# Output projection of a hybrid decoder layer from seven products of half-size blocks

## The chip, the cores and the metric

The kernel runs on one core of a Trainium2 chip. A core has TensorE (matrix products into eight PSUM banks of 128 x 512 floats), VectorE and ScalarE (elementwise work, both reach PSUM), GpSimd (elementwise work in SBUF) and SyncE, whose queue (SP) issues the DMA transfers here. Each engine works through its own queue in order; semaphores order the queues among each other. The metric is the device time of one execution in microseconds.

## The reference

One layer on x of 512 x 1024 floats: RMSNorm, one input projection, four mLSTM heads and eight attention heads, and an output projection with the residual:

```
h = rmsnorm(x, norm_w);  proj = h @ w_in            # 1024 x 4616
y_ml = rmsnorm(sigmoid(o) * mlstm(q, k, v, i, f)) * silu(z)     # 512 x 512, 4 heads of 128
y_at = moba_attention(q, k, v) * silu(z)                        # 512 x 512, 8 heads of 64
out  = x + concat([y_ml, y_at], -1) @ w_out         # (512 x 1024) @ (1024 x 1024)
```

The last line is what the change rewrites.

## The kernel before

All large products are made from float32 split in two parts: hi is the value rounded to fp32r, lo is the rest. `mm3` (L343) adds three products into a bank: hi x hi, hi x lo, lo x hi. A right side of 512 columns is the widest one.

Weights come in pieces of 128 x 1024 (two k-tiles of 512 columns). `load_w` (L221) issues a piece's DMA into one of three `raw` tiles; `g_split` (L237) makes `whi` on ScalarE (a cast) and `wlo` on VectorE (raw minus hi), with six tiles of each. The main stream emits the projections in the order z, aq, ak, av, qk0, qk1, mo, mv, az; everything beside it (evacuation, attention, mLSTM heads, weight splits) is written as Python generators that the class `Plan` resumes when an estimate of time says that what they wait for is there. So the order in each engine's queue comes from that planner.

The end of the program: the four mLSTM heads (`g_mlstm`) are normalised on VectorE, with a small power on GpSimd (tile `mst`), transposed on TensorE, and `put_y` makes hi and lo of the left side in `br` tiles. `ev_z` does the same for the attention half in `cv`, then `xh` and `xl`. The output projection (`out_mm`, L848) runs over two halves of 512 columns, four row blocks of 128 and eight k-tiles: 4 x 8 x 3 = 96 products of 512 columns for each half, and the last row block of the second half in two pieces of 256 columns, so that its last add and store are short. `ev_out` adds the residual, loaded to `tq` and `tk`, and issues the store:

```
    for ks in ((0, 1, 2, 3), (4, 5, 6, 7)):
        for t in range(NT):
            for k in ks:
                out_mm(ps4[t], 0, t, k)
```

Of the kernel before, what the change touches and what calls it, by code (L numbers as in the profile page):

```python
# [10 lines left out]
F32 = mybir.dt.float32  # L11
F32R = mybir.dt.float32r
# [4 lines left out]
P = 128  # L17
D = 1024
S = 512
# [32 lines left out]
class Engine:  # L52
    """Issues to one engine and keeps an estimate of when it gets through."""

# [74 lines left out]


@with_exitstack
def hybrid_layer(ctx: ExitStack, tc: tile.TileContext, xT, x, w_in, w_out, smalls, out):
# [48 lines left out]

    # the table of Silu and the clock of TensorE come up while the first loads run
    rstdb = sb("rstdb", [P, S])
# [9 lines left out]

    # ---- weights, in pieces of two k-tiles
    pieces = []
    off = 0
    for name, cols in _chunks():
        n = len(cols)
        for kk in range(4):
            pieces.append((name, kk, n, w_in, off))  # L200
# [9 lines left out]
    W = {}  # L210
    raws = {}
    nload, nsplit = [0], [0]

    def src_ap(i):
        _, _, n, src, o = pieces[i]
        return bass.AP(tensor=src.tensor, offset=src.offset + o, ap=[[2 * n, P], [1, 2 * n]])

    def pair(t, n):
        return t[:, :2 * n].rearrange("p (k n) -> p k n", k=2)

    def load_w(dst=None, between=None):  # L221
        i = nload[0]
        if i >= len(pieces) or (dst is None and i - max(nsplit[0], 5) >= 3):
# [11 lines left out]
        raws[i] = pair(dst, n)  # L235

    def g_split(i, copy=act.copy, parts=1):  # L237
        name, kk, n, _, _ = pieces[i]
        raw = raws.pop(i)
# [7 lines left out]
        load_w()  # L247

    def split_w():
        i = nsplit[0]  # L250
        if i < len(pieces):
            nsplit[0] += 1
            plan.add(g_split(i), rank=1)
# [17 lines left out]

    # ---- long-lived tiles
    sz = sb("sz", [P, NT, 512])
# [79 lines left out]
    def feat_mm(ps, name, f, k):  # L353
        hi, lo = need_w(name, k // 2)
        fs = slice(f * P, (f + 1) * P)
        mm3(ps, hi[:, k % 2, fs], lo[:, k % 2, fs], xh[:, k], xl[:, k], k == 0, k == KT - 1)

    def main_bank():
        plan.until(banks.ok)
        return banks.get()  # L360

    def group(g, mul, evac):
# [61 lines left out]

    # ---- gates of the mLSTM heads
    def g_rstdb():
# [66 lines left out]

    # ---- attention
    pts = {}
# [146 lines left out]

    # ---- mLSTM
    yh, yl = {}, {}

    def put_y(f, src, scale, t_=0.0):
        hi, lo = (br.get(), br.get()) if f < 4 else (xh[:, f - 4], xl[:, f - 4])
        if scale is None:
            yield act.copy(hi, src)
            t_ = dve.tensor_tensor(lo, src, hi.bitcast(F32), op=ALU.subtract)  # L650
        else:
            yield act.activation(hi, src, AF.Copy, scale=scale)
            t_ = dve.scalar_tensor_tensor(lo, src, scale, hi.bitcast(F32), op0=ALU.mult, op1=ALU.subtract)
        yh[f], yl[f] = hi, lo
        yield t_

    def g_mlstm(h):
# [99 lines left out]
        yield plan.now + SLACK  # L757
        for t_ in put_y(h, ps, sm[:, C_MN + h:C_MN + h + 1]):
            yield t_
# [4 lines left out]
    def ev_z(f):  # L764
        z = cv[f // 2][:, f % 2]

        def ev(ps):
            t_ = dve.tensor_tensor(z, ps, rstdb, op=ALU.mult)
            banks.put(t_, ps)
            yield t_  # L770
            yield act.activation(z, z, AF.Silu)
            t_ = dve.tensor_tensor(z, z, ot[:, f], op=ALU.mult)
            yield when(lambda: have["proj"], t_)
            for t_ in put_y(4 + f, z, None):
                yield t_
        return ev

    have["proj"] = 0

    # ---- main stream  # L780
    psz = [[banks.get() for _ in range(2)] for _ in range(NT)]
# [60 lines left out]
    tok_chunk("mv", lambda t: ev_scale(mv[:, t, :, 0:128], t, "mv", MLH))  # L842
    plan.until(lambda: have["silu"] == 3)
    for f in range(4):
        group(f, lambda ps, k: feat_mm(ps, "az", f, k), ev_z(f))
    have["proj"] = 1

    def out_mm(ps, half, t, k, c0=0, c1=512):  # L848
        plan.until(lambda: k in yh)
        hi, lo = need_w(f"wo{half}", k // 2)  # L850
        ts = slice(t * P, (t + 1) * P)
        mm3(ps[:, :c1 - c0], yh[k][:, ts], yl[k][:, ts], hi[:, k % 2, c0:c1], lo[:, k % 2, c0:c1],
            k == 0, k == KT - 1)

    xres = []
    plan.until(lambda: have["y"] == MLH)
    for half in range(2):
        r = tk if half else tq
        for t in range(NT):
            nc.sync.dma_start(r[:, t], x[t * P:(t + 1) * P, half * 512:half * 512 + 512])  # L860
        xres.append([r[:, t] for t in range(NT)])

    def ev_out(half, t, c0=0, c1=512):
        def ev(ps):
            o = xres[half][t][:, c0:c1]
            t_ = dve.tensor_tensor(o, ps[:, :c1 - c0], o, op=ALU.add)
            banks.put(t_, ps)
            nc.sync.dma_start(out[t * P:(t + 1) * P, half * 512 + c0:half * 512 + c1], o)
            yield t_
        return ev  # L870

    ps4 = [main_bank() for _ in range(NT)]
    for ks in ((0, 1, 2, 3), (4, 5, 6, 7)):
        for t in range(NT):
            for k in ks:
                out_mm(ps4[t], 0, t, k)
                plan.run()
        for _ in range(2):
            split_w()
    for t in range(NT):  # L880
        plan.add(ev_out(0, t)(ps4[t]), rank=0, ready=plan.now + SLACK)
    for t in range(NT):
        cols = ((0, 512),) if t < NT - 1 else ((0, 256), (256, 512))
        for c0, c1 in cols:
            ps = main_bank()
            for k in range(KT):
                out_mm(ps, 1, t, k, c0, c1)
                plan.run()
            plan.add(ev_out(1, t, c0, c1)(ps), rank=0, ready=plan.now + SLACK)
    plan.until(lambda: not plan.programs)  # L890

# [35 lines left out]
```

## Time and profile before

| what | us |
|---|---|
| median of 3 runs (310.26 to 310.55) | 310.38 |
| span of the profiled execution | 308.8 |
| TensorE busy | 303.2 |
| VectorE busy | 185.8 |
| ScalarE busy | 150.2 |
| GpSimd busy | 58.3 |

The span is that of one profiled execution, from its first instruction to its last; the runs are timed without a profile. Busy time of TensorE counts pipelined products, so it says that TensorE never waits, not that it is at its peak. All helpers of VectorE, ScalarE and GpSimd record line 75; they are told apart by their tiles.

### The profile page before, as it was taken

The page shows a single profiled execution, that of the slowest core. Times are in us where ns is not written, and L with a number is a line of the kernel's source. Part 1 is how long each engine was busy: PE and PEld are TensorE (multiplying, and loading weights), DVE is VectorE, ACT ScalarE, POOL GpSimd, SP SyncE. Part 2 cuts the span into 40 slices and gives each one's busy share as a digit, 9 for nine tenths or more (in the row PEclk, how much of TensorE's full clock was granted, in tenths as well). Part 3 has the DMA queues.
Part 4 walks back from the last instruction along what each step waited for, and adds up shares of the span by engine and source line. Part 5 has one row for each costly group of instructions (what it writes and reads, how often), then busy time and mean ns, then how long its engine had stood idle before and what let it go on. Part 6 is the DMA issues. An engine that isn't in the chain of part 4 may idle for free.

```text
span 308.8 us, 4284 instructions
## 1 busy us (share of the span) xinstructions
PE 303.2 (98%) x1594; PEld 248.2 (80%) x1594; DVE 185.8 (60%) x395; ACT 150.2 (49%) x271; POOL 58.3 (19%) x94
## 2 busy tenths in 40 slices
PE   7999999999999999999999999999999999999995
PEld 3999888778888868886886888688889978788885
DVE  4892458935456549999627995501568999714111
ACT  3372754314365671775439356899763237420000
POOL 3000164262501800450150005110000060000000
PEclk9999999999999999999999999999999999999999
DMA  7997122141410410132103021400252102832101
GB/s 198 394 412 300 68 69 75 63 137 49 155 70 0 168 39 9 60 128 78 68 2 137 0 83 55 138 0 2 93 176 73 44 24 72 306 135 102 36 34 68
DMA packets 10821, 31.80 MB, mean 103 GB/s; under 512 B 1328, under 2 KB 1584, under 8 KB 10800
## 3 DMA queue, kind: packets, MB, share of 16 engines
q1 hardware_dynamic: 10800, 31.53, 28.8%
q8 instruction: 12, 0.20, 0.3%
q14 instruction: 9, 0.07, 0.1%
HBM read 29.42 MB, written 2.10 MB: 102 GB/s over the span
## 4 chain that ended last, share of the span: by engine, by line
PE 95%; DMA 2%; SPq 1%; DVE 1%; ACT 0%; issue 0%
PE bank L173 89%; PE bank L177 6%; DMA tq<-in_xT_dram 2%; ACT xh L75 0%; DVE wlo L75 0%; SPq L306 0%; DVE xl L75 0%; SPq L234 0%; SPq L232 0%; DVE tk L75 0%; SPq L230 0%; SPq L180 0%
## 5 line engine op out<-in xcount | busy, mean ns | idle before, releaser
L173 PE MATMUL bank<-whi,xh 128*128 128x512 f32 (+2 forms) x260 | 86.4, 367 | 0.7 <-DVE whi L75 0.7
L173 PE MATMUL bank<-wlo,xh 128*128 128x512 f32 (+2 forms) x260 | 85.1, 363 | 0.2 <-DVE wlo L75 0.2
L173 PE MATMUL bank<-whi,xl 128*128 128x512 f32 (+2 forms) x260 | 85.2, 363 | 0.0
L75 DVE TENSOR_TENSOR wlo<-raw,whi 128x1024 fp32r<-128x1024 f32 x39 | 48.0, 1241 | 10.8 <-ACT whi L75 9.2
L173 PEld LDWEIGHTS bank<-whi,xh 128*128 128x128 f32 x260 | 45.1, 188 | 8.7 <-ACT xh L75 1.1
L173 PEld LDWEIGHTS bank<-whi,xl 128*128 128x128 f32 x260 | 45.0, 188 | 8.1
L173 PEld LDWEIGHTS bank<-wlo,xh 128*128 128x128 f32 x260 | 45.1, 188 | 7.9 <-DVE wlo L75 0.6
L75 ACT CAST whi<-raw 128x1024 fp32r<-128x1024 f32 x39 | 40.8, 1048 | 19.8 <-PE bank L173 11.5
L173 PE MATMUL bank<-xh,whi 128*128 128x512 f32 x96 | 40.9, 426 | 0.0
L173 PE MATMUL bank<-xh,wlo 128*128 128x512 f32 x96 | 37.9, 395 | 0.0
L173 PE MATMUL bank<-xl,whi 128*128 128x512 f32 x96 | 37.7, 393 | 0.0
L75 POOL TENSOR_SCALAR b<-b,rec 128x128 f32<-128x128 f32 (+3 forms) x32 | 18.9, 612 | 84.6 <-DVE rec L75 67.1
L75 ACT ACTIVATE br<-bank,sm 64x512 fp32r<-64x512 f32 (+1 forms) x28 | 19.1, 684 | 14.7 <-DVE br L75 9.7
L173 PEld LDWEIGHTS bank<-xh,whi 128*128 128x128 f32 x96 | 18.2, 190 | 4.5 <-issue 2.1
L173 PE MATMUL bank<-whi,br 128*128 128x512 f32 (+1 forms) x72 | 21.4, 370 | 0.0
L173 PEld LDWEIGHTS bank<-xh,wlo 128*128 128x128 f32 x96 | 18.0, 188 | 4.2
L75 ACT ACTIVATE b<-b,mn 128x128 f32<-128x128 f32 (+3 forms) x32 | 17.6, 553 | 7.6 <-DVE mn L75 7.5
L173 PEld LDWEIGHTS bank<-xl,whi 128*128 128x128 f32 x96 | 18.2, 189 | 2.5
L75 DVE SCALAR_TENSOR_TENSOR br<-bank,sm,br 64x512 fp32r<-64x512 f32 (+1 forms) x20 | 15.0, 749 | 5.9 <-ACT br L75 5.6
L75 DVE CUSTOM_DVE_ANT_0 b<-bank,b 128x128 f32<-128x128 f32 (+3 forms) x32 | 14.2, 488 | 5.5 <-PE bank L173 5.4
L173 PEld LDWEIGHTS bank<-whi,br 128*128 128x128 f32 x72 | 13.1, 188 | 2.6
L177 PEld LDWEIGHTS bank<-ident,b 128*128 128x128 f32 (+1 forms) x104 | 12.3, 140 | 3.4 <-issue 0.4
(141 smaller groups left out, 374.1 us busy)
## 6 DMA issues: line engine op xcount, KB each, us to landing
raw<-in_w_in_dram SPq DMA_DIRECT2D x31, 512.0 KB, 3.2
raw<-in_w_out_dram SPq DMA_DIRECT2D x8, 512.0 KB, 3.5
b<-in_w_in_dram SPq DMA_DIRECT2D x3, 520.0 KB, 7.5
tq<-in_xT_dram SPq DMA_DIRECT2D x4, 256.0 KB, 5.4
tk<-in_xT_dram SPq DMA_DIRECT2D x4, 256.0 KB, 7.8
ot<-in_x_dram SPq DMA_DIRECT2D x2, 512.0 KB, 9.1
cv<-in_x_dram SPq DMA_DIRECT2D x2, 512.0 KB, 9.9
tq<-in_x_dram SPq DMA_DIRECT2D x4, 256.0 KB, 5.8
```

Of the source, the lines that this page charges most:

```text
L75: fn(out, *args, **kw)
L173: nc.tensor.matmul(out_, lhsT=lhsT, rhs=rhs, start=start, stop=stop, skip_group_check=True)
L177: nc.tensor.transpose(out_, in_, idn)
```

## The change

The 512 x 1024 by 1024 x 1024 product is cut in four blocks on each side (left: rows in two halves r, k in two halves; right: k in two halves r, columns in two halves c) and made from seven products of half-size blocks, p5, p1, p2, p6, p3, p7 and p4 in that order. Each is 256 rows by 512 k by 512 columns: 2 row blocks x 4 k-tiles x 3 = 24 products of 512 columns. The right sides are weight blocks or sums of two of them; the sums are made on GpSimd, 128 x 1024 at a time, and then split in hi and lo as before. The left sides are blocks of y, or sums and differences of them: differences of the mLSTM and the attention half on VectorE (`b<-tq,cv`), three more combinations on GpSimd (L1117), and each is split in hi and lo. Each product is added to or subtracted from the residual's tiles (`res`, named `b` in the rows) on VectorE; some banks collect two products first. Output weights are loaded in blocks, some of them twice. `Stage` is a list scheduler: it takes tasks with an engine, a cost and what they come after, and emits them by start and longest tail; the whole last stage goes through it. The first two products' weights, and the p5 left side, are prepared by the planner as before.

```diff
+class Stage:
...
+        for t in order:
+            t["tail"] = t["cost"] + max([t["lat"] + u["tail"] for u in t["next"]], default=0.0)
...
+                start = max(free.get(e, 0.0), min(t["ready"] for t in can))
+                t = max((t for t in can if t["ready"] <= start), key=lambda t: (t["tail"], -t["n"]))
...
-    off = 0
-    for half in range(2):
-        for kk in range(4):
-            pieces.append((f"wo{half}", kk, 512, w_out, off))
-            off += P * 2 * 512
...
+    PRODS = [("p5", [(0, 0), (0, 1)]), ("p1", [(0, 0)]), ("p2", [(0, 0), (1, 0)]), ("p6", [(0, 0), (1, 1)]),
+             ("p3", [(0, 1), (1, 1)]), ("p7", [(1, 1)]), ("p4", [(1, 0), (1, 1)])]
...
+        if name in OVER:
+            src = B.pop((*OVER[name], u))
+            pair_ = [B.get(b, src) for b in blocks]
+            t_ = pool.tensor_tensor(src, *pair_, op=ALU.subtract if name == "p6" else ALU.add)
...
+        yield act.copy(hi, src)
+        t_ = dve.tensor_tensor(lo, src, hi.bitcast(F32), op=ALU.subtract)
...
-            t_ = dve.scalar_tensor_tensor(lo, src, scale, hi.bitcast(F32), op0=ALU.mult, op1=ALU.subtract)
...
+        yield dve.tensor_tensor(lo(h), yml[:, h, H[1]], hi(h).bitcast(F32), op=ALU.subtract)
...
+    CHAIN = {"p5": ("B", (1, 1, ADD, False)), "p1": ("A", (0, 0, ADD, False)),
+             "p2": ("1", (0, 0, ADD, True)), "p6": ("A", (0, 1, SUB, False)),
+             "p3": ("B", (0, 1, ADD, True)), "p7": ("A", (1, 1, SUB, True)),
+             "p4": ("A", (1, 0, ADD, True))}
...
+        last = PARTS[q] = st.add("PE", 3 * 231.0 * (q[4] - q[3]) / 512, part(*q), [last], lat=0.0)
...
+        BL[tag] = st.add("SP", 1450.0, dma(dst, w_src(*blk)), after, lat=2500.0)
...
+                sums[name, u] = t_ = st.add("POOL", 2250.0, lambda src=src, w2=w2, op=op: nc.gpsimd.tensor_tensor(src, src, w2, op=op), dep)
...
+            last = st.add("ACT", 1050.0, f_hi, dep)
+            lows[name, u] = t_ = st.add("DVE", 1240.0, f_lo, [last])
...
+        h_ = st.add("ACT", n, lambda: nc.scalar.copy(hi, src), [*dep, *war])
+        l_ = st.add("DVE", n + 10, lambda: nc.vector.tensor_tensor(lo, src, hi.bitcast(F32), op=SUB), [h_, *war])
...
+    t_ = st.add("DVE", 690.0, vec(z3, ps3, rstdb, ALU.mult), at=300.0)
...
+        x1.append(st.add("DVE", 420.0, vec(xav[:, f], yml[:, f, H[0]], y_at[f][:, H[0]]), z))
+        xs1.append(split("p1", f, xav[:, f], [x1[f]]))
+        split("p2", f, y_at[f][:, H[0]], z)
+        split("p4", f, y_at[f][:, H[1]], z)
...
+        r_ = st.add("POOL", 1200.0, gps(xrv[:, ks], yml[:, ks, H[1]], xav[:, ks]), x1[ks])
+        s_ = split("p6", ks, xrv[:, ks], [r_])
...
+        c_ = st.add("POOL", 1200.0, gps(xav[:, ks], yml[:, ks, H[0]], yml[:, ks, H[1]]), [r_, *xs1[ks]])
...
+        e_ = st.add("POOL", 1200.0, gps(xrv[:, ks], xrv[:, ks], cv[u][:, :, H[1]]), [s_, zdone])
...
+        t_ = st.add("DVE", 80 + 1.2 * (c1 - c0), ev_prod(bank[key, a][:, c0:c1], d, op), [*deps, RL[r, c, a], old])
```

What stands on VectorE in the output stage before: the low parts of the attention half (`xl`), weight splits (`wlo`), and adds from banks into the residual.

```order
L75 SCALAR_TENSOR_TENSOR br_83<-bank_87,sm,br_84 128x512
L75 TENSOR_TENSOR cv_132<-bank_93,rstdb 128x512
L75 TENSOR_TENSOR xl<-cv_131,xh 128x512 x2
L75 TENSOR_TENSOR xl<-cv_132,xh 128x512
L75 TENSOR_TENSOR cv_132<-cv_132,ot 128x512
L75 TENSOR_TENSOR xl<-cv_132,xh 128x512
L75 TENSOR_TENSOR wlo<-raw,whi 128x1024 x2
L75 TENSOR_TENSOR tq<-bank_91,tq 128x512
```

And now, from the last head's low part on, the first twelve of 37 rows up to the last weight split:

```order
L75 TENSOR_TENSOR br_81<-tq,br_85 128x256 x2
L1114 TENSOR_TENSOR b_3_72<-tq,cv_131 128x256 x2
L1114 TENSOR_TENSOR cv_132<-bank_91,rstdb 128x512
L1123 TENSOR_TENSOR br_84<-b_3_72,br_82 128x256 x2
L1114 TENSOR_TENSOR b_3_72<-tq,cv_132 128x256
L1123 TENSOR_TENSOR xl<-cv_131,xh 128x256
L1114 TENSOR_TENSOR cv_132<-cv_132,ot 128x512
L1123 TENSOR_TENSOR xl<-cv_131,xh 128x256
L1114 TENSOR_TENSOR b_3_72<-tq,cv_132 128x256
L1123 TENSOR_TENSOR br_83<-b_3_72,br_79 128x256
L1104 TENSOR_TENSOR wlo<-raw,whi 128x1024
L1123 TENSOR_TENSOR br_83<-b_3_72,br_79 128x256
```

Differences of left sides, more low parts at half width and ten weight splits stand on VectorE now where four splits and a few low parts stood.

GpSimd at the end of the program before; `mst` is the small power of each head, and nothing follows the fourth:

```order
L75 AFFINE_SELECT b_1_70<-b_1_70 128x512
L75 TENSOR_SCALAR mst<-mst 128x4
L75 TENSOR_TENSOR mst<-mst,mhalf 128x4
```

And now, from the last head's power on (the first product's two sums stand ahead of the powers):

```order
L75 TENSOR_TENSOR mst<-mst,mhalf 128x4
L75 TENSOR_TENSOR raw<-raw 128x1024
L1117 TENSOR_TENSOR b_4_73<-tq,b_3_72 128x512
L1117 TENSOR_TENSOR b_3_72<-tq 128x512
L1092 TENSOR_TENSOR sz<-sz,raw 128x1024
L1092 TENSOR_TENSOR raw<-raw,sz 128x1024
L1092 TENSOR_TENSOR raw<-raw,vbuf 128x1024
L1117 TENSOR_TENSOR b_4_73<-tq,b_3_72 128x512
L1092 TENSOR_TENSOR vbuf<-vbuf,sz 128x1024
L1092 TENSOR_TENSOR tk<-tk,vbuf 128x1024
```

Fourteen sums of 128 x 1024 or 128 x 512 follow the heads' powers where nothing did; the last five of them are not shown.

## Rows read from the trace of the kernel before

**Rows 1.** The page: span, and busy time of TensorE.

```profile
span 308.8 us, 4284 instructions
PE 303.2 (98%) x1594; PEld 248.2 (80%) x1594; DVE 185.8 (60%) x395; ACT 150.2 (49%) x271; POOL 58.3 (19%) x94
```

**Rows 2.** The chain that ended last, merged: start us, us, what.

```profile
258.58 46.75 PE bank L173 x225
...
305.35 0.42 DVE tk L75
```

**Rows 3.** Stretches: us; PE, PEld, DVE, ACT, POOL busy (x); PEclk; DMA share; GB/s.

```profile
260.00:270.00 10.00, 10.00 (x44) 7.98 (x43) 8.13 (x11) 4.00 (x6) 0.00 (x0) 1.00 0.85 283
...
290.00:300.00 10.00, 10.00 (x47) 8.22 (x46) 1.02 (x2) 0.00 (x0) 0.00 (x0) 1.00 0.14 52
300.00:309.00 9.00, 5.32 (x45) 5.11 (x44) 1.22 (x3) 0.00 (x0) 0.00 (x0) 0.96 0.16 58
```

**Rows 4.** Timeline of TensorE, output stage's first and last product: start us, us, what.

```profile
260.51 0.39 PE L173 MATMUL bank<-whi,br 128*128 128x512 f32 x1
...
305.04 0.28 PE L173 MATMUL bank<-whi,xl 128*128 128x256 f32 x1
```

**Rows 5.** Groups by line and shape from 225 us: busy us, mean ns.

```profile
L75 DVE TENSOR_TENSOR wlo<-raw,whi 128x1024 fp32r<-128x1024 f32 x10 | 12.0, 1219 | 0.3 <-ACT whi L75 0.3
L75 ACT CAST whi<-raw 128x1024 fp32r<-128x1024 f32 x8 | 8.3, 1046 | 5.5 <-issue 3.0 <-DMA raw<-in_w_out_dram 2.1 <-PE bank L173 0.5
L75 DVE TENSOR_TENSOR tk<-bank,tk 128x512 f32<-128x512 f32 x3 | 2.1, 692 | 12.3 <-PE bank L173 12.3
L75 DVE TENSOR_TENSOR tk<-bank,tk 128x256 f32<-128x256 f32 x2 | 0.8, 425 | 4.6 <-PE bank L173 4.6
```

**Rows 6.** Timeline of VectorE in the output stage.

```profile
261.32 0.75 DVE L75 SCALAR_TENSOR_TENSOR br<-bank,sm,br 128x512 fp32r<-128x512 f32 x1
...
262.58 1.89 DVE L75 TENSOR_TENSOR xl<-cv,xh 128x512 fp32r<-128x512 f32 x3
...
283.64 2.35 DVE L75 TENSOR_TENSOR wlo<-raw,whi 128x1024 fp32r<-128x1024 f32 x2
```

**Rows 7.** Timelines of VectorE and GpSimd where both read SBUF.

```profile
104.46 1.73 DVE L75 TENSOR_TENSOR wlo<-raw,whi 128x1024 fp32r<-128x1024 f32 x1 [1.35 <-PE bank L173]
104.48 0.63 POOL L75 TENSOR_SCALAR b<-dist 128x512 f32<-128x512 f32 x1
105.20 1.47 POOL L75 TENSOR_SCALAR b<-dist 128x512 f32<-128x512 f32 x1
118.57 2.33 DVE L75 SCALAR_TENSOR_TENSOR cv<-xp,sm,cv 128x512 f32<-128x512 f32 x3
131.84 2.99 DVE L75 SCALAR_TENSOR_TENSOR cv<-xp,sm,cv 128x512 f32<-128x512 f32 x3 [0.45 <-ACT cv L75]
132.14 1.13 POOL L75 TENSOR_SCALAR b<-b,rec 128x512 f32<-128x512 f32 x1
158.35 0.63 POOL L75 TENSOR_SCALAR b<-dist 128x512 f32<-128x512 f32 x1
```

**Rows 8.** The same two timelines where neither was stretched.

```profile
49.46 1.65 POOL L75 TENSOR_TENSOR rq<-rq,mhalf 128x8 f32<-128x8 f32 x1
49.88 1.23 DVE L75 TENSOR_TENSOR wlo<-raw,whi 128x1024 fp32r<-128x1024 f32 x1 [0.26 <-ACT whi L75]
81.41 0.63 POOL L75 TENSOR_SCALAR b<-dist 128x512 f32<-128x512 f32 x1
81.48 0.69 DVE L75 TENSOR_TENSOR tk<-bank,rq 128x512 f32<-128x512 f32 x1 [1.91 <-POOL rq L75]
```

**Rows 9.** Timeline of GpSimd, the first head's power near the end.

```profile
246.66 0.20 POOL L75 TENSOR_SCALAR mst<-mst 128x4 f32<-128x4 f32 x1 [39.66 <-DVE mst L75]
```

**Rows 10.** Timeline of TensorE, the program's first products (on zeros).

```profile
1.24 3.90 PE L191 MATMUL bank<-rstdb 128*128 128x512 bf16 x10 [1.24 <-DVE warm L187]
```

**Rows 11.** The page's DMA issues: count, KB each, us from issue to landing.

```profile
raw<-in_w_out_dram SPq DMA_DIRECT2D x8, 512.0 KB, 3.5
```

More of the change, by code (lines that the diff above doesn't have):

```diff
@@ L128, in put, with __init__, add, run @@
         self.free.extend([when, t] for t in tiles)
+class Stage:
+    def __init__(self):
+        self.tasks = []
+    def add(self, eng, cost, fn, after=(), at=0.0, lat=220.0):
+        t = {"eng": eng, "cost": cost, "fn": fn, "after": [a for a in after if a], "at": at, "lat": lat, "n": len(self.tasks)}
+        self.tasks.append(t)
+        return t
+    def run(self, clocks):
+        for t in self.tasks:
+            t["next"], t["left"], t["ready"] = [], len(t["after"]), t["at"]
+        last = None
+        for t in self.tasks:
+            for a in t["after"]:
+                a["next"].append(t)
+        order, seen = [], {}
+        def visit(t):
+            if seen.get(t["n"]):
+                return
+            seen[t["n"]] = 1
+            for u in t["next"]:
+                visit(u)
+            order.append(t)
+        for t in self.tasks:
+            visit(t)
+        for t in order:
+            t["tail"] = t["cost"] + max([t["lat"] + u["tail"] for u in t["next"]], default=0.0)
+        free, done, todo = dict(clocks), [], {t["n"]: t for t in self.tasks}
+        while todo:
+            best = None
+            for e in {t["eng"] for t in todo.values()}:
+                can = [t for t in todo.values() if t["eng"] == e and not t["left"]]
+                if not can:
+                    continue
+                start = max(free.get(e, 0.0), min(t["ready"] for t in can))
+                t = max((t for t in can if t["ready"] <= start), key=lambda t: (t["tail"], -t["n"]))
+                if best is None or start < best[0]:
+                    best = (start, t)
+            start, t = best
+            del todo[t["n"]]
+            free[t["eng"]] = start + t["cost"]
+            done.append((start, t))
+            for u in t["next"]:
+                u["left"] -= 1
+                u["ready"] = max(u["ready"], start + t["cost"] + t["lat"])
+        for start, t in done:
+            t["start"] = start
+            t["fn"]()
+        return done
 @with_exitstack
@@ L210, in hybrid_layer @@
     W = {}
+    NREG = sum(p[3] is w_in for p in pieces)
     raws = {}
@@ L252, in split_w @@
             nsplit[0] += 1
-            plan.add(g_split(i), rank=1)
+            plan.add(g_split(i) if i < NREG else g_osplit(i), rank=1)
     def need_w(name, kk):
@@ L757, in g_mlstm @@
         yield plan.now + SLACK
-        for t_ in put_y(h, ps, sm[:, C_MN + h:C_MN + h + 1]):
+        yield when(lambda: have["S"] == MLH)
+        if "p5" not in X:
+            X["p5"] = two([br.get() for _ in range(2)]), two([br.get() for _ in range(2)])
+        for t_ in put_ml(h, ps, sm[:, C_MN + h:C_MN + h + 1]):
             yield t_
@@ L857, in hybrid_layer @@
[L857 to L889, printed above, removed]
@@ L890, in hybrid_layer, with ev_keep @@
-    plan.until(lambda: not plan.programs)
+    for j in range(len(LOADS)):
+        plan.add(g_load(j), rank=1)
+    def ev_keep(ps):
+        zlast.append(ps)
+        yield 0.0
+    for f in range(NT):
+        group(f, lambda ps, k: feat_mm(ps, "az", f, k), ev_z(f) if f < 3 else ev_keep)
+    plan.until(lambda: have["y"] == MLH and have["zat"] == 3 and zlast and ("p1", 1) in W and (1, 0, 0) in B)
+    st = Stage()
+    ADD, SUB = ALU.add, ALU.subtract
+    NAMES = [n for n, _ in PRODS]
+    xa, xr = b5.get()[:, 0:1024], b5.get()[:, 0:1024]
@@ new lines, in hybrid_layer, with part, fn @@
+    bank = {}
+    for key in "BA1":
+        for a in range(2):
+            bank[key, a] = main_bank()
+    PARTS = {}
+    seq = []
+    for name in NAMES:
+        wide = [(a, k, 0, 512) for k in range(4) for a in range(2)]
+        if name in ("p7", "p4"):
+            wide = [(a, k, c0, c1) for a in range(2)
+                    for c0, c1 in (((0, 256), (256, 512)) if name == "p4" and a else ((0, 512),)) for k in range(4)]
+        seq += [(name, *w) for w in wide]
+    def part(name, a, k, c0, c1):
+        def fn():
+            key = "1" if (name, c0) == ("p4", 256) else CHAIN[name][0]
+            hi, lo = W[name, k // 2]
+            xs = X[name]
+            ts = slice(a * P, (a + 1) * P)
+            mm3(bank[key, a][:, c0:c1], xs[0](k)[:, ts], xs[1](k)[:, ts], hi[:, k % 2, c0:c1], lo[:, k % 2, c0:c1],
+                k == 0 and (name in ("p5", "p1", "p2") or key == "1"), k == 3)
+        return fn
@@ new lines, in hybrid_layer, with parts, before @@
+    last = None
+    for q in seq:
+        last = PARTS[q] = st.add("PE", 3 * 231.0 * (q[4] - q[3]) / 512, part(*q), [last], lat=0.0)
+    def parts(name, **kw):
+        names = ("name", "a", "k", "c0")
+        return [t for q, t in PARTS.items() if q[0] == name and all(q[names.index(n)] == v for n, v in kw.items())]
+    def before(task, consumers):
+        for c in consumers:
+            c["after"].append(task)
+    rooms = [t[:, 1024 * u:1024 * u + 1024] for t in (flat(sz), vbuf, flat(tk), flat(ot)) for u in range(2)]
@@ new lines, in dma, with w_src, load, load_res @@
+    def dma(out_, in_):
+        return lambda: nc.sync.dma_start(out_, in_)
+    def w_src(r, c, u):
+        return bass.AP(tensor=w_out.tensor, offset=w_out.offset + (c * 4 + 2 * r + u) * P * 1024, ap=[[1024, P], [1, 1024]])
+    BT, BL = {}, {}
+    def load(tag, blk, dst, after=()):
+        BT[tag] = dst
+        BL[tag] = st.add("SP", 1450.0, dma(dst, w_src(*blk)), after, lat=2500.0)
+    def load_res(r, c):
+        for a in range(2):
+            t_ = 2 * r + a
+            RL[r, c, a] = st.add("SP", 730.0, dma(res[r, c, a], x[t_ * P:(t_ + 1) * P, c * 512:c * 512 + 512]), lat=2500.0)
@@ new lines, in vec, with gps, split @@
+    def vec(out_, a, b, op=SUB):
+        return lambda: nc.vector.tensor_tensor(out_, a, b, op=op)
+    def gps(out_, a, b, op=SUB):
+        return lambda: nc.gpsimd.tensor_tensor(out_, a, b, op=op)
+    def split(name, ks, src, dep, war=()):
+        hi, lo = X[name][0](ks), X[name][1](ks)
+        n = 410.0 if isinstance(ks, int) else 650.0
+        h_ = st.add("ACT", n, lambda: nc.scalar.copy(hi, src), [*dep, *war])
+        l_ = st.add("DVE", n + 10, lambda: nc.vector.tensor_tensor(lo, src, hi.bitcast(F32), op=SUB), [h_, *war])
+        for k in ([ks] if isinstance(ks, int) else range(ks.start, ks.stop)):
+            before(l_, parts(name, k=k))
+        return l_
@@ new lines, in hybrid_layer @@
+    for name in NAMES:
+        key, (r, c, op, end) = CHAIN[name]
+        for a in range(2):
+            if name == "p4" and a:
+                result(name, r, c, op, a, 256, 512, key, parts("p7", a=a), False)
+                result(name, r, c, op, a, 0, 256, key, parts(name, a=a, c0=0), True)
+                result(name, r, c, op, a, 256, 512, "1", parts(name, a=a, c0=256), True)
+                continue
+            t_ = result(name, r, c, op, a, 0, 512, key, parts(name, a=a), end)
+            if name in AFTER:
+                before(t_, parts(AFTER[name], a=a))
+            if name == "p2" and a:
+                before(t_, parts("p4", a=a, c0=256))
```

172 lines of the change are left out of this document (144 added, 28 removed).

## The prediction

> **What bounds the kernel now.** I read the page first, then the chain, then a table by stretches, then single rows of the last 50 us. The page gives TensorE 303.2 of 308.8 us busy [rows 1], and the chain's last long piece is one uninterrupted run of products from 258.58 to 305.33, followed only by one add on VectorE and its store [rows 2]. The table says the same of the stage that the change rewrites: from 260 on TensorE is busy in every stretch, at a granted clock of 1.00 until it stops, while VectorE's 8 us in 10 fall to 1 and GpSimd does nothing [rows 3]. So the output stage is bound by its count of products. Its first product starts at 260.51 and its last ends at 305.32 [rows 4]: 44.8 us for 192 products of 512 columns (the last row block's 48 products have 256 columns and count half), that is 0.2334 us each. After it come 3.5 us until the span's end at 308.8 (add, store, landing), which any version pays. The page's execution has a span of 308.8 us; the median of the runs is 310.38, so 1.6 us are added to a span to get a time.
>
> **Products.** Seven half-size products of 24 each are 168, so 24 go: 24 x 0.2334 = 5.6 us less. If TensorE never waited, the stage would take 168 x 0.2334 = 39.2 us. Ahead of the stage one weight split of 1.22 us now stands between the last heads' normalisations on VectorE, and TensorE's transposes wait for these; I charge half of it, 0.6 us (0 to 1.2). With TensorE alone the change is therefore worth -5.6 + 0.6 = -5.0.
>
> **What VectorE gets.** By the order it has 42 instructions from the last head's low part to its last weight split, where before it had 20 in the whole rest of the program. Durations start to start: a split of 128x1024 takes 1.13, with the hand-overs 1.14 (two in 2.35 [rows 6] less the 1.22 of one [rows 5]), a 512 wide one 0.60 (three in 1.89 [rows 6] less the 0.69 of one); a 256 wide one lasts 0.425 where a 512 wide one lasts 0.692 [rows 5], so 0.33 start to start (estimate). The list: 10 weight splits = 11.4; 7 of 512 columns with two operands in SBUF = 4.2; 18 of 256 columns, two operands in SBUF = 5.9; 7 of 512 columns that read a PSUM bank = 4.2. Sum 25.7 us. If nothing else held it, VectorE would be through its last split at about 261.7 + 25.7 = 287.4, some 7 us before the seventh product starts (261.1 + 144 x 0.2334 = 294.7), and all of it would be hidden under the products.
>
> **What GpSimd gets, and the port.** Thirteen of the sums fall in the same stretch: 7 of 128x1024 and 6 of 128x512, all reading SBUF twice. The trace of before has no such sum. What it has is GpSimd reading SBUF beside VectorE, and there the two take turns [rows 7]. At 104.46 a weight split, 1.22 elsewhere, lasted 1.73; a GpSimd instruction of 0.63 began 0.02 later and ran at full speed; the next one, again 0.63 alone (158.35), lasted 1.47 and ended 0.48 after the split. So the split waited for the first and the second waited for the split. At 131.84 three VectorE instructions with both operands in SBUF took 2.99 instead of the 2.33 of the same three at 118.57, and the first of the GpSimd ones between them, at 132.14, 1.13 instead of 0.63. Where VectorE reads a PSUM bank and a small operand, both ran at full speed (81.41 and 81.48) [rows 8]. So I take the two engines' SBUF reads as exclusive, instruction by instruction, in order of arrival. Then 35 of VectorE's 42 instructions (21.5 us) and all 13 sums share one resource.
>
> The Trainium skill (SBUF — State Buffer, "Who interferes with whom") states this as a rule that speaks against the change: a VectorE instruction with two SBUF inputs and a GpSimd instruction that reads SBUF exclude each other for a whole instruction, and the first to come goes first. The rows at 104.46 agree. The row at 49.46 agrees only in part: a GpSimd power over 128x8 lasted 1.65 us and a weight split that began at 49.88 kept its 1.23 [rows 8], so what is held seems to be the reading, not the instruction; a sum reads to its end, so by either reading it holds.
>
> Price of a sum. Lower end: one pass over 1024 elements, twice the 0.63 of a GpSimd instruction over 512 [rows 7], 1.26 us. Upper end: two operands read one after the other, 2.52 us. A gain is no end here, since an instruction more on an engine that waits for the port gives nothing back. I take 2.25 (1.2 for 512 columns), near the upper end, because both operands have to be read and because the change's own list of costs, which charges 2250 and 1200 ns, is within 2% of the rows wherever a row exists (cast 1050 for 1.046, weight split 1240 for 1.219, add 690 for 0.692) [rows 5].
>
> The Trainium skill (GPSIMD Engine Reference, "Elementwise — side-by-side cycle accounting") gives 4497 ns for a two-input add of 2048 elements a partition; an estimate from that page is 2.25 us for 1024, which would give the same sum as below.
>
> Sum for the stage: GpSimd 7 x 2.25 + 6 x 1.2 = 22.95; VectorE's two-operand instructions 21.5; together 44.45 us through one door. VectorE's list starts where the last head's low part stood before, 261.32 [rows 6], later by one more weight split ahead of it (1.14), earlier by three left-side splits at half width (3 x 0.33), and later by what one sum costs that falls on the heads' last steps (0 to 1.4, 0.2 taken): 261.7. Its last weight split is then through at 261.7 + 44.45 = 306.15. The seven PSUM readers and waits for ScalarE lie under GpSimd's turns. Behind that split VectorE has four adds (4 x 0.60 = 2.4) of which the fourth frees the bank that the seventh product writes; then its 24 products, 24 x 0.2334 = 5.6; with 0.2 for hand-overs the last product ends at 314.35, 9 us later than before. With 3.5 behind it the span is 317.85, and with 1.6 the time is **319.5**. TensorE then stands still for some 14 of 53 us: its waits are for the low parts of the second product's left side and for the weight splits of the third, fifth and seventh.
>
> What else moves. SP issues 12 loads of output weights instead of 8, 2 MB more; a load lands in 3.5 us [rows 11] and the DMA engines, at 0.85 of their time in the stage's first 10 us, are down to 0.14 later [rows 3], so nothing, as long as each is issued 5 us ahead, which the stage's length gives. ScalarE's casts (ten of 1.05, eighteen and more of 0.4) are under 25 us in a stretch of 40: nothing, since VectorE's queue behind them is longer. The first product's two sums and one more stand on GpSimd's queue ahead of, or between, the heads' small instructions; GpSimd had idled 39.66 us before the first of these [rows 9], so the first two cost nothing; the third may hold the port up to 2.25 at the last head, which is the 0 to 1.4 above.
>
> **The rivals.**
> Rival A, faster: long sums don't hold the port, or hold it only at their start as the power did. For: that row [rows 8]. Against: every GpSimd instruction of 512 elements in rows 7. Then VectorE is through in time, TensorE never waits: 310.4 - 5.0 = 305.4.
> Rival B, the same door at a lower price: at 1.26 and 0.63 a sum the door needs 12.6 + 21.5 = 34.1, 10.35 less than above, and the time is 309.1. Loss turns to gain where the sums take 9.1 less than above, that is where one of 1024 costs 1.39 us. Against it: two operands in the time of one.
> Rival C, slower still, one mechanism: the clock. In the last stretch, where products end at 305.32, the granted clock is 0.96, so it fell from full to half (1.2 GHz) while TensorE stood idle [rows 3]; the first products of the program, after an idle start, took 0.39 us each [rows 10] instead of 0.2334. My sum has waits of 3 to 4 us on TensorE in the stage. What runs slow behind them is mostly taken from TensorE's own idle time; if it reached the seventh product it would cost up to 24 x 0.16 = 3.8: 323.3. With the full clock and sums at 2.52 and 1.26 it is 321.7.
> That the change does not do what it says is out: the order shows the products gone.
>
> **How the numbers follow.** Forecast (exclusive turns, sums of about 1.95 to 2.4): 0.62, 316 to 321. Rival C above 321: 0.08. Cheaper or shorter turns, 311 to 316: 0.08. Within 0.2% of before (0.6 us, about what a measurement can tell from no change): 0.03. Faster: 0.19, of which A is 0.15 and B at its low end 0.04. So slower 0.78, same 0.03, faster 0.19. The range leaves out A and the far end of C: 309.0 to 322.5.
>
> **What would show it.** In the profile after: GpSimd sums of 2.2 to 2.3 us where alone and up to 3.3 where they waited; weight splits of 2 to 3.3 us beside them instead of 1.22, and 256 wide ones of up to 2.5 instead of 0.42; TensorE idle some 14 us between 265 and 310, waiting for VectorE; the last weight split at about 306. I am wrong if the splits keep 1.22 beside sums (A), if sums alone take under 1.4 (B), or if TensorE waits for something else than VectorE, a DMA first of all.

## The result and the profile after

The changed kernel takes 321.21 us (median of 4 runs, 321.15 to 321.36) and the kernel before, on the same chip, 310.47 (310.26 to 310.81): a ratio of 1.034, 95% interval 1.033 to 1.036. It is slower by 10.7 us, though TensorE has 24 products fewer. Predicted were 319.5 us and a range of 309.0 to 322.5.

The page after, its span, busy times and the chain's shares by engine (to be read against [rows 1] and [rows 2]):

```profile
span 319.4 us, 4302 instructions
PE 303.0 (95%) x1558; PEld 244.8 (77%) x1558; DVE 223.3 (70%) x426; ACT 162.8 (51%) x295; POOL 93.7 (29%) x110
...
PE 72%; DVE 20%; issue 4%; DMA 2%; SPq 1%; ACT 0%; DVEq 0%
```

TensorE is still busy for 303.0 us, which looks like before, but the span is 10.6 us longer, and a fifth of the chain is now VectorE's. Where that happened, the stretches of after say (us; PE, PEld, DVE, ACT, POOL busy (x); PEclk; DMA share; GB/s), against [rows 3]:

```profile
260.00:270.00 10.00, 10.00 (x44) 7.89 (x42) 10.00 (x13) 4.21 (x11) 6.34 (x4) 1.00 1.00 367
270.00:280.00 10.00, 3.68 (x10) 2.28 (x9) 10.00 (x6) 5.95 (x12) 9.58 (x5) 0.83 0.43 171
280.00:290.00 10.00, 6.82 (x26) 5.13 (x26) 10.00 (x10) 4.11 (x5) 4.77 (x3) 0.90 0.00 0
290.00:300.00 10.00, 9.83 (x40) 7.60 (x38) 10.00 (x9) 3.77 (x4) 7.18 (x3) 0.93 0.01 2
300.00:310.00 10.00, 8.66 (x35) 6.49 (x35) 10.00 (x14) 0.00 (x0) 0.00 (x0) 1.00 0.07 27
```

Before, TensorE was full to the end and VectorE sank to 1 us in 10. Now VectorE is "busy" 10.00 in 10 in all five stretches, yet from 270 to 280 it gets through 6 instructions where 14 are usual at the end. TensorE stood still for 11.0 us (6.32 + 3.18 + 0.17 + 1.34), and GpSimd is the engine that is new there. What TensorE waited for from 260 on (line and releaser: us in total, times, longest):

```profile
PE bank L230 <- DVE br L1123: 6.3, 2, 4.5
PE bank L230 <- DVE wlo L1104: 3.6, 2, 3.2
PE bank L230 <- DVE b L1152: 1.3, 1, 1.3
```

L1123 makes the low parts of left sides, L1104 those of the weights, L1152 are the adds that free the banks: all VectorE. Its own timeline (start, us, what), against [rows 5] and [rows 6], is stretched where GpSimd's sums (L1092 of weight blocks, L1117 of left sides) run:

```profile
261.33 0.75 DVE L75 TENSOR_TENSOR br<-tq,br 128x256 fp32r<-128x256 f32 x2
...
266.50 2.89 DVE L1114 TENSOR_TENSOR cv<-cv,ot 128x512 f32<-128x512 f32 x1
269.31 2.58 DVE L1123 TENSOR_TENSOR xl<-cv,xh 128x256 fp32r<-128x256 f32 x1
271.82 2.55 DVE L1114 TENSOR_TENSOR b<-tq,cv 128x256 f32<-128x256 f32 x1
274.29 0.41 DVE L1123 TENSOR_TENSOR br<-b,br 128x256 fp32r<-128x256 f32 x1
274.63 2.29 DVE L1104 TENSOR_TENSOR wlo<-raw,whi 128x1024 fp32r<-128x1024 f32 x1
...
291.15 1.27 DVE L1152 TENSOR_TENSOR b<-b,bank 128x512 f32<-128x512 f32 x2
292.34 0.54 DVE L1123 TENSOR_TENSOR xl<-cv,xh 128x256 fp32r<-128x256 f32 x1
292.81 3.42 DVE L1104 TENSOR_TENSOR wlo<-vbuf,whi 128x1024 fp32r<-128x1024 f32 x1
...
306.57 1.21 DVE L1104 TENSOR_TENSOR wlo<-ot,whi 128x1024 fp32r<-128x1024 f32 x1
307.71 3.99 DVE L1152 TENSOR_TENSOR b<-b,bank 128x512 f32<-128x512 f32 x7
```

```profile
266.26 2.59 POOL L1092 TENSOR_TENSOR sz<-sz,raw 128x1024 f32<-128x1024 f32 x1
268.80 2.81 POOL L1092 TENSOR_TENSOR raw<-raw,sz 128x1024 f32<-128x1024 f32 x1
271.56 2.53 POOL L1092 TENSOR_TENSOR raw<-raw,vbuf 128x1024 f32<-128x1024 f32 x1
...
291.30 1.29 POOL L1117 TENSOR_TENSOR b<-b,cv 128x512 f32<-128x512 f32 x1 [5.57 <-DVE xl L1123]
292.57 2.58 POOL L1092 TENSOR_TENSOR tk<-tk,sz 128x1024 f32<-128x1024 f32 x1
295.10 3.38 POOL L1092 TENSOR_TENSOR ot<-ot,vbuf 128x1024 f32<-128x1024 f32 x1
```

VectorE's timeline shows no wait in all this: the wait is inside the duration. A 256 wide subtraction of 0.41 us lasts 2.55 (at 271.82) when it begins 0.26 after a sum, and ends 0.28 after it. The sum at 295.10 lasts 3.38, because the split at 292.81 had been waiting when it came. The adds at 291.15, which read a bank and one operand in SBUF, run at full speed (two in 1.27) beside the sum at 291.30.

### The profile page after: what moved, and what is told of

It is laid out like the page before. It is cut to its first block, busy times and chain, and to the rows that moved or that the text cites. A ratio compares the mean times of both kernels' runs of the same rounds, so it can differ in the third digit from the quotient of the medians.

```text
span 319.4 us, 4302 instructions
## 1 busy us (share of the span) xinstructions
PE 303.0 (95%) x1558; PEld 244.8 (77%) x1558; DVE 223.3 (70%) x426; ACT 162.8 (51%) x295; POOL 93.7 (29%) x110
## 4 chain that ended last, share of the span: by engine, by line
PE 72%; DVE 20%; issue 4%; DMA 2%; SPq 1%; ACT 0%; DVEq 0%
PE bank L230 67%; PE bank L234 5%; DVE wlo L1104 4%; DVE b L75 3%; DVE xl L1123 3%; DMA tq<-in_xT_dram 2%; DVE wlo L75 2%; DVE b L1152 2%; DVE b L1114 1%; DVE br L1123 1%; DVE cv L1114 1%; DVE den L75 1%; DVE cv L75 1%; DVE mst L75 1%; ACT xh L75 0%
## 5 line engine op out<-in xcount | busy, mean ns | idle before, releaser
L75 DVE TENSOR_TENSOR wlo<-raw,whi 128x1024 fp32r<-128x1024 f32 x35 | 43.2, 1238 | 10.5 <-ACT whi L75 8.9
L75 ACT CAST whi<-raw 128x1024 fp32r<-128x1024 f32 x35 | 36.7, 1048 | 15.7 <-PE bank L230 13.7
L230 PE MATMUL bank<-whi,br 128*128 128x512 f32 x48 | 16.6, 423 | 6.4 <-DVE br L1123 6.3
L75 ACT ACTIVATE br<-bank,sm 64x512 fp32r<-64x512 f32 x24 | 16.4, 683 | 11.8 <-DVE br L75 9.7
L230 PEld LDWEIGHTS bank<-whi,br 128*128 128x128 f32 x48 | 9.3, 199 | 9.9 <-DVE br L1123 7.9
L75 DVE SCALAR_TENSOR_TENSOR br<-bank,sm,br 64x512 fp32r<-64x512 f32 x16 | 12.0, 749 | 5.9 <-ACT br L75 5.6
```

Source lines behind the costliest of these rows:

```text
L75: fn(out, *args, **kw)
L230: nc.tensor.matmul(out_, lhsT=lhsT, rhs=rhs, start=start, stop=stop, skip_group_check=True)
```

## The experiments

Each is timed against the kernel before on the same chip (310.3 to 310.6). The theory, "turns": a sum on GpSimd and a VectorE instruction with both operands in SBUF exclude each other, so both lists add up.

**No sums.** The stage without GpSimd's sums, its order kept:

```
-  nc.gpsimd.tensor_tensor(src, src, w2, op=op)          # weight blocks
-  gps(xrv[:, ks], yml[:, ks, H[1]], xav[:, ks])         # left sides, and two more such
+  None
```

> The changed kernel with the output stage's fourteen GpSimd sums left out (eight of weight blocks, six of left sides); the splits behind them read one operand of each sum, so the output is not the reference's. Everything else, the order included, stays. Turns theory (GpSimd's sums and VectorE's instructions with two operands in SBUF exclude each other): VectorE's 42 instructions need 25.7 us and are through at about 287.5 us, before the seventh product needs them, so TensorE does not wait and the time is that of 168 products, 305.4 us. Rival, order: it is the order of VectorE's list, or the first products' start, and not the sums, that keeps TensorE waiting: 315 to 321 us. Rival, late sums (TensorE waits because the sums themselves come late, not because of the port) also says 305.4; the next two kernels tell it from the first.

305.14 us (305.06 to 305.52), ratio 0.983 [0.981, 0.984]: within 0.3 us of the 168 products without a wait. Its stretches show TensorE full, which settles that neither the order nor the loads cost anything:

```profile
270.00:280.00 10.00, 10.00 (x45) 8.10 (x44) 8.40 (x14) 6.66 (x9) 0.00 (x0) 1.00 0.41 164
280.00:290.00 10.00, 10.00 (x45) 8.08 (x44) 9.25 (x12) 2.11 (x2) 0.00 (x0) 1.00 0.01 2
```

**Sums that nobody reads.** The same sums into a spare tile:

```
-  nc.gpsimd.tensor_tensor(src, src, w2, op=op)
+  nc.gpsimd.tensor_tensor(xr, src, w2, op=op)           # left sides likewise; splits read one operand
```

> The same fourteen sums in the same places of GpSimd's list, but written to a tile that nobody reads; the splits read one operand each, as in the kernel without sums, so the output is not the reference's. Turns theory: nobody waits for a sum, but each still takes its turn with VectorE's reads; the shared list stays 44 to 46 us long and the time within 316 to 322 us. Late sums: with nobody waiting for a sum the time falls to 305.4 us, as without them. Weight splits beside sums last 2 to 3.4 us by the first, 1.22 by the second.

322.71 us (322.31 to 323.10), ratio 1.039 [1.037, 1.041]. That nobody waits for them saves nothing: late sums are out, and it is their running that costs. It lies 0.7 us above the range that I gave for turns. TensorE's last wait, 6.4 us for a weight split of the third product, was over at 290.54 here; the nine products behind it that ran at the half clock (0.43 us instead of 0.23, 1.7 us together) had no later wait to be hidden in.

**Fills instead of sums.** GpSimd is nearly as busy (1.97 us for two fills of 1024 elements, where a sum alone takes 2.4) and is still waited for, but reads nothing:

```
-  nc.gpsimd.tensor_tensor(src, src, w2, op=op)
+  for _ in range(2): nc.gpsimd.memset(src, 0.5)         # left sides likewise
```

> Each sum replaced by two fills of the same tile with a constant on GpSimd, for which the splits still wait; the output is not the reference's. The fill of 36x512 in the program's start takes 0.515 us, so two of 1024 elements are estimated at 2.1 us and two of 512 at 1.05: GpSimd's own load and the waits for it stay, 21 us, but nothing is read from SBUF. Turns theory, where only reads take turns: no turns, weight splits keep 1.22 us and the time is 305.4 to 307 us. If any GpSimd instruction on SBUF takes the turn, writes too: 44 us of shared list, 317 to 321. Late sums: 317 to 321 with weight splits of 1.22.

305.21 us (304.97 to 306.23), ratio 0.984 [0.982, 0.985]. VectorE's and GpSimd's timelines run side by side with nothing stretched: a split between fills keeps 1.22, a 512 wide subtraction 0.68.

```profile
265.29 1.22 DVE L1110 TENSOR_TENSOR wlo<-raw,whi 128x1024 fp32r<-128x1024 f32 x1
...
267.44 0.68 DVE L1129 TENSOR_TENSOR xl<-b,xh 128x512 fp32r<-128x512 f32 x1
```

```profile
264.21 1.98 POOL L1079 MEMSET sz<- 128x1024 f32 x2
266.12 3.90 POOL L1079 MEMSET raw<- 128x1024 f32 x4
```

So it is the reading that excludes. The Trainium skill (SBUF — State Buffer, "Who interferes with whom") says the same: VectorE's second SBUF operand meets a GpSimd instruction that reads SBUF, and not one that only writes it; this trace agrees.

**All sums on VectorE.**

```
-  st.add("POOL", 2250.0, ... nc.gpsimd.tensor_tensor(src, src, w2, op=op)
+  st.add("DVE", 1240.0, ... nc.vector.tensor_tensor(src, src, w2, op=op)     # left sides: 690.0
```

> The whole computation, with the output stage's fourteen sums on VectorE instead of GpSimd, put in order by the same scheduler with VectorE's durations. Turns theory: a sum costs VectorE 1.14 us (0.60 for the 512 wide) instead of 2.25 (1.2) of the shared list, so the list is 21.5 + 8.0 + 3.6, and the 4.2 us of bank readers no longer lie beside anything: 37.3 us instead of 44.45 to 46.45, and the time 312 to 314 us, faster than the changed kernel though VectorE has more to do. Rival, VectorE simply has too much work: 11.6 us more on the engine that TensorE waits for, 321 + 11.6 = 333 us; or, if GpSimd and VectorE work side by side as separate engines, any price between 321 and 333.

309.34 us (309.23 to 309.56), ratio 0.996 [0.995, 0.998]: 11.9 us faster than the changed kernel with 12.7 us more work (8 x 1.14 + 6 x 0.60) on the engine that TensorE waits for, and a little faster than the kernel before. The list was near what I expected (from 260.51 to 298.60, 38.1 us against 37.3); the time was some 3 us under the expectation because of what stands behind it. VectorE's timeline near its end:

```profile
293.65 0.68 DVE L1152 TENSOR_TENSOR b<-b,bank 128x512 f32<-128x512 f32 x1
...
296.53 0.68 DVE L1152 TENSOR_TENSOR b<-b,bank 128x512 f32<-128x512 f32 x1
...
297.46 1.21 DVE L1104 TENSOR_TENSOR wlo<-ot,whi 128x1024 fp32r<-128x1024 f32 x1
```

Here the adds that free the seventh product's banks stand ahead of the last weight split; in the changed kernel four stood behind it (307.71). So from the last split to the last product's end it is 5.2 us here (303.78 less 298.60) and 8.5 there: my "time = list + 274.9" held for one order of the tail only.

**Left sums alone on VectorE.** As the last one, for the six sums of left sides.

> The whole computation, with only the six 512 wide sums of left sides moved to VectorE; the eight sums of weight blocks stay on GpSimd. Turns theory: the shared list is 7 x 2.25 on GpSimd and 21.5 + 6 x 0.60 on VectorE, 40.9 us instead of 44.45, so 3.6 us less than the changed kernel: 317.6 us, between it (321.2) and the kernel with all sums on VectorE (309.3). Rival, the left sums alone are what TensorE waits for (they feed the second, fourth and fifth product, and are the ones for whose operands GpSimd waits): nearly all of the 11.9 us between those two kernels comes back, 310 to 311. Rival, only the weight sums count: no change, 321.

319.10 us (318.48 to 320.21), ratio 1.028 [1.026, 1.030]: a part comes back, as turns say and neither rival does, but 2.1 us instead of 3.6. Seven of the eight weight sums now ran nearly back to back from 261.5 to 280.6, each letting little more than one small VectorE instruction through, and TensorE's wait moved together into one of 9.4 us for a low part of the second product's left side. Behind it nine products ran at the half clock (1.7 us more), and TensorE did not wait again, so it was this wait and not the end of VectorE's list (304.76) that set the time.

**Half as long sums.** Each 1024 wide sum in two:

```
-  nc.gpsimd.tensor_tensor(t, t, w, op=op)
+  for c in (slice(0, 512), slice(512, 1024)): nc.gpsimd.tensor_tensor(t[:, c], t[:, c], w[:, c], op=op)
```

> The changed kernel with each 1024 wide sum on GpSimd cut into two of 512 elements, so that a turn lasts half as long; the whole computation. Turns theory, where the sum of all turns counts: 7 x (2 x 1.2) + 6 x 1.2 = 24.0 instead of 22.95 in the list: 321 to 323, no faster than the changed kernel. Rival, what costs is the length of a turn (short VectorE instructions caught behind a long sum): the waits are halved and the time falls to 313 to 318. If VectorE gets several instructions in between the halves, sums come later but splits earlier.

320.74 us (320.57 to 321.01), ratio 1.033 [1.031, 1.034]: 0.5 us less than the changed kernel, just under what I expected, and far from 313 to 318. It is the total of the turns that costs, not their length.

**Filled waits.** 31 products more, ahead of the three longest waits:

```
+  for _ in range({("p1", 0, 2): 13, ("p1", 0, 3): 9, ("p2", 0, 2): 9}.get((name, a, k), 0)):
+      mm(spare, xs[0](k)[:, ts], hi[:, k % 2, c0:c1])
```

> The changed kernel with 31 products more on TensorE, into a bank that nobody reads, put right ahead of the three places where it waited longest: 13 (3.0 us at 0.2334) ahead of the wait of 4.9 us, 9 (2.1 us) ahead of that of 2.4, 9 ahead of that of 3.6. They fit into the waits, so that TensorE stands still for no more than 2 us there, and are meant to keep its granted clock at 1.00, where in the changed kernel 13 products behind these waits took 0.43 us instead of 0.23 (2.6 us). Turns theory: VectorE's shared list sets the pace and the slow products only ran where TensorE would have waited anyway: 321.2, within 0.5. Rival, the fallen clock carries a part of the loss: down to 318.6. If the clock falls all the same, the run says nothing.

321.50 us (321.35 to 321.62), ratio 1.035 [1.034, 1.037]. The clock did stay up:

```profile
270.00:280.00 10.00, 7.42 (x32) 5.37 (x31) 10.00 (x6) 5.86 (x12) 9.57 (x5) 1.00 0.48 189
280.00:290.00 10.00, 8.88 (x38) 6.90 (x39) 10.00 (x10) 4.47 (x6) 5.21 (x3) 1.00 0.00 0
290.00:300.00 10.00, 8.93 (x38) 6.65 (x36) 10.00 (x9) 3.77 (x4) 7.15 (x3) 1.00 0.01 2
```

PEclk is 1.00 where it was 0.83 to 0.93, 31 more products fit in, and the time is the same. In the changed kernel the fallen clock carries nothing of the loss: behind its slow products TensorE waits for VectorE again, the last time at 310.32.

**The kernel before with sums.** Thirteen sums in the second half of its output stage:

```
+  if t == 1:
+      for n in [1024] * 7 + [512] * 6:
+          nc.gpsimd.tensor_tensor(flat(ot)[:, :n], flat(tq)[:, :n], flat(sz)[:, :n], op=ALU.add)
```

> The kernel before, with thirteen sums on GpSimd added (seven of 128x1024, six of 128x512, as in the changed kernel's stage, into a tile that nobody reads) in the second half of its output stage, where VectorE has four to five adds left that read a bank and one operand in SBUF. Turns theory: such an add takes no turn, keeps 0.69 us, and TensorE reads on undisturbed: 310.4, no change; the sums themselves show their price alone, 2.2 to 2.3 and 1.1 to 1.2 us. Rival, a sum on GpSimd costs by itself, through SBUF or the weight loads of TensorE, whatever VectorE does: 311.5 or more, with products above 0.2334 us beside them.

313.53 us (313.43 to 313.74), ratio 1.010 [1.008, 1.011]. I had expected no change, and had overlooked two weight splits that stand in this stretch, the row at 283.64 of [rows 6]. The same place now, and TensorE's waits in the stage:

```profile
283.69 6.43 DVE L75 TENSOR_TENSOR wlo<-raw,whi 128x1024 fp32r<-128x1024 f32 x2
```

```profile
PE bank L173 <- DVE wlo L75: 2.5, 2, 1.7
```

Two splits of 2.35 became 6.43, each held up by one sum, and TensorE waited for both. The five adds that ran among the sums kept 0.69, and outside these waits products kept their pace. So the miss speaks for turns: two caught instructions were enough for 2.9 us. Sums that met nobody (from 291 on) lasted 2.4 and 1.29 us.

**Six weight sums by adding transfers.** A transfer from GpSimd's queue adds the second block onto the first; the two differences and the left sums stay on GpSimd:

```
-  t_ = st.add("POOL", 2250.0, lambda ...: nc.gpsimd.tensor_tensor(src, src, w2, op=op), dep)
+  t_ = st.add("POOL", 1000.0, lambda ...: nc.gpsimd.dma_start(src, w_src(*blk), accum_op=ADD), dep, lat=4000.0)
```

> The whole computation, with six of the eight sums of weight blocks (those of the second, third and seventh product) made by transfers that add onto the block already there, issued from GpSimd's queue; the two differences and the six left sums stay on GpSimd. Turns theory: a transfer takes no turn with VectorE, so the shared list is 21.5 + 2 x 2.25 + 6 x 1.2 = 33.2 us, and with the changed kernel's relation (44.45 us of list for 319.5, 46.45 measured for 321.2, so about 274.9 + list) the time is 308.1; 305.4 (168 products without a wait) is the floor. Rival, late transfers: a plain load lands in 3.5 us; if an adding one takes 8 us or more, or holds GpSimd's queue for that long, TensorE waits for it instead of for VectorE: 312 to 321, with the waits put down to DMA.

312.80 us (312.80 to 313.47), ratio 1.008 [1.007, 1.009]: 8.4 us faster than the changed kernel, 4.7 slower than I expected. No wait is put down to DMA. VectorE's list ran from 260.61 to 297.15, 36.5 us against 33.2, as I had again put all bank readers beside the sums, and the first add came at 283.73, when all eight sums were over. But the list's end did not set this time: the last product ended 10.7 us behind it, at 307.83. TensorE waited once, 4.0 us, for a low part of the second product's left side; ahead of that stood two VectorE instructions that had each waited 2.1 to 2.2 us for one of the two differences left on GpSimd. Behind the wait twelve products ran at the half clock, 0.43 us each instead of 0.23, together 2.3 us, and as no long wait followed, these count in full. The stretch (columns as before) and two rows of TensorE:

```profile
270.00:280.00 10.00, 5.99 (x18) 4.45 (x17) 10.00 (x7) 4.31 (x6) 10.00 (x8) 0.74 1.06 300
```

```profile
275.74 1.22 PE L230 MATMUL bank<-whi,br 128*128 128x512 f32 x2 [4.01 <-DVE br L1126]
...
278.04 0.63 PE L230 MATMUL bank<-wlo,xh 128*128 128x512 f32 x1
```

So my "time = list + 274.9" had no ground here: what was late was one early instruction, not the list.

**And no sum on GpSimd.** As the last one, the rest on VectorE.

> As the last one, with the two differences of weight blocks and the six left sums on VectorE, so that GpSimd makes no sum in the stage. Turns theory: VectorE alone has 21.5 + 2 x 1.14 + 6 x 0.60 + 4.2 of bank readers = 31.6 us, through at 261.2 + 31.6 = 292.8, ahead of the seventh product's need at 294.7: no wait on TensorE, 305.4 us (305 to 307), which would be faster than both kernels. Rival, late transfers: as there, 309 us or more, with waits on TensorE put down to DMA or to splits that waited for one.

308.33 us (307.49 to 309.52), ratio 0.994 [0.992, 0.996]: faster than both kernels, but above the floor. VectorE had room; it idled 3.07 us ahead of a split whose block came by an adding transfer. TensorE waited once, 1.8 us, for a cast of a left side that stood in ScalarE's queue behind a cast that had waited 4.18 us for another adding transfer. The rows in VectorE's and ScalarE's timelines, and in the table of DMA issues of the stage (count, KB each, us from issue to landing) the first of these transfers beside the plain load of the same tile:

```profile
273.12 1.23 DVE L1107 TENSOR_TENSOR wlo<-sz,whi 128x1024 fp32r<-128x1024 f32 x1 [3.07 <-ACT whi L1103]
```

```profile
280.63 1.05 ACT L1103 CAST whi<-tk 128x1024 fp32r<-128x1024 f32 x1 [4.18 <-DMA tk<-in_w_out_dram]
```

```profile
sz<-in_w_out_dram SPq DMA_DIRECT2D x2, 512.0 KB, 6.4
...
sz<-in_w_out_dram POOLq DMA_DIRECT2D x1, 512.0 KB, 9.4
```

**Four adding transfers**, for the fifth and seventh product; the third product's sums are on VectorE too (`if name in ("p2", "p6")` in place of `"p6"`, `lat=7500.0`).

> As the version with six sums by adding transfers and none on GpSimd, but the two sums of the third product, whose transfers land last before they are needed, are on VectorE; four adding transfers remain (fifth and seventh product). Late transfers as the cause of the 1.8 us that TensorE still waited there: that wait goes, and as VectorE's list of 31.6 + 2 x 1.14 = 33.9 us ends at 295.1, about when the seventh product needs it (294.7), the time is 305.4 to 306.5, below that version's 307.5 to 309.5 and less scattered. Rival, VectorE's list is what held it: 2.3 us more on VectorE, 309 to 310.

305.33 us (304.95 to 306.05), ratio 0.983 [0.982, 0.985]: 5.3 us faster than the kernel before and 15.9 than the changed one, at the floor that the products set. TensorE waits nowhere in the stage, though VectorE is as full as in the changed kernel: it does 14 instructions where that did 6.

```profile
270.00:280.00 10.00, 10.00 (x44) 8.09 (x44) 10.00 (x14) 5.71 (x7) 1.69 (x2) 1.00 1.06 257
280.00:290.00 10.00, 10.00 (x44) 8.08 (x43) 10.00 (x14) 5.60 (x8) 0.03 (x1) 1.00 0.46 124
```

**Two adding transfers**, for the seventh product alone.

> Only the two sums of the seventh product by adding transfers, all others on VectorE: a list of 36.2 us there, through at 297.4, 2.7 later than needed; by the turns theory between the kernel with all sums on VectorE (37.3 us of list, 309.3) and the product-bound 305.4: 307.5 to 309. If transfers, and not VectorE, are what is late, this one is the fastest of the three: 305.4 to 306.

307.83 us (307.63 to 308.30), ratio 0.991 [0.990, 0.993], between the two as expected. With all sums on VectorE, then two, four and six by transfer, the times are 309.34, 307.83, 305.33 and 308.33: first VectorE's list is what is late, at six the transfers are.

## Why the prediction was right, and where it was off

The mechanism held: products go, VectorE's own list would have fitted, and the shared reading of SBUF makes one list of VectorE's and GpSimd's. The rivals fell: sums hold the port to their end (A), at a price near the upper bound (B), and the clock fell as C says but cost nothing in this kernel, as C's own sentence on idle time allowed. Step by step:

- **Products**, -5.0 if TensorE never waits: 305.4 predicted; without sums 305.14. Right, with the 0.6 for the split ahead (the stage's first product starts at 261.19 instead of 260.51).
- **VectorE's list unblocked**, 25.7 us and over before it is needed: with fills it is 26.1 us of work (260.40 to 288.81, less 2.34 idle), and TensorE never waits. The start, 261.7, was 261.33 in the changed kernel, 0.4 earlier.
- **Price of a sum**, 2.25 and 1.2: seven VectorE instructions that waited for one whole 1024 wide sum lasted 2.13 to 2.21 more than alone, mean 2.18 (2.55 less 0.42 at 271.82 is one), four that waited for a 512 wide one 1.06 to 1.09. A little too dear; 7 x 2.18 + 6 x 1.08 = 21.7 instead of 22.95. The sum's own 2.4 us where it met nobody is no more than 7% above the 2.25 estimated from the Trainium skill (GPSIMD Engine Reference, "Elementwise — side-by-side cycle accounting").
- **"The seven PSUM readers lie under GpSimd's turns"**: this term was mis-sized. Of their 4.2 us only some 1.3 ran beside sums (at 262.67 and 291.15). GpSimd was through at 298.48, and idle for 5.57 us before 291.30 as it waited for VectorE; for the last 9 us VectorE worked alone. That is 2.9 us more, less the 1.2 of the cheaper sums; the earlier start (0.4) and the list's own 0.4 cancel. The last weight split was through at 307.71, not 306.15. The same term made the list too short once more in the run with six transfers, though there the list's end did not set the time.
- **The tail**, four adds and 24 products, 8.2 us: 8.5 (307.71 to the last product's end at 316.19); from there to the span's end 3.2 instead of 3.5, and 1.8 instead of 1.6 from span to time. Together 1.56 + 0.3 - 0.3 + 0.2, the 1.7 us between 319.5 and 321.2.
- **Waits of TensorE**: on the low parts and weight splits that were named. From its first product to the end of its last (261.19 to 316.19) the stage took 15.8 us more than 39.2, where 14 were predicted. Of these 11.0 are the idle time above and 2.6 went into products at the half clock (13 at 0.43 instead of 0.23 us), all between waits that VectorE ended; the rest lies around the waits, where a product of 0.39 us has no neighbour to overlap with (estimate).
- **SP and ScalarE at nothing**: right; no wait of TensorE in the stage is put down to either.

## What to carry to other kernels

Work moved to an idle engine is free only if it doesn't share what the busy one reads through: here VectorE was faster with the sums in its own list (1.14 us each) than with GpSimd making them beside it (2.18 us of standing still each). Add the two lists up, let only those instructions lie side by side that the order really puts there, and look at every instruction in the stretch: a pair of them was enough for 2.9 us. And find the wait behind which TensorE never waits again: only the products that ran slow behind that one cost time here (2.3 us in the first run with six transfers, nothing in the changed kernel). Where a sum's operand comes from DRAM anyway, an adding transfer takes it off both engines, if it is issued some 10 us ahead.

## What the hardware showed beyond that

The wait for the port appears in no list of waits, only as a longer duration, and as 10.00 of 10 busy: the count of instructions in a stretch (6 against 14) gave it away. In the two runs with six of them an adding transfer of 512 KB took 5.4 to 10 us from issue to landing amid the stage's other loads (medians, where a tile has two), a plain one 3.0 to 16.1, and GpSimd 0.9 to 1.2 us to issue.

Who comes first is not always who goes first. In the kernel with the left sums on VectorE, a sum that showed from 261.50, while VectorE was at a weight split, lasted 3.85 us, 1.45 more than one that met nobody, and four VectorE instructions with two SBUF operands that began after it kept their durations; it got through when VectorE came to a bank reader at 263.00. VectorE's and GpSimd's rows:

```profile
261.66 0.75 DVE L75 TENSOR_TENSOR br<-tq,br 128x256 fp32r<-128x256 f32 x2
262.33 0.75 DVE L1114 TENSOR_TENSOR b<-tq,cv 128x256 f32<-128x256 f32 x2
263.00 0.68 DVE L1114 TENSOR_TENSOR cv<-bank,rstdb 128x512 f32<-128x512 f32 x1
```

```profile
261.50 3.85 POOL L1092 TENSOR_TENSOR sz<-sz,raw 128x1024 f32<-128x1024 f32 x1 [3.91 <-DMA sz<-in_w_out_dram]
```

At 274.51 in the changed kernel a sum in the same position got in after one instruction, and the weight split at 274.63 waited for it (2.29 us). What decides between the two stays open; no run here tells it.
